# Moving the GLU, the gates and the SSM branch of a hybrid decoder layer, and the first expert's VectorE work

## The chip, the cores and the metric

One NeuronCore of a Trainium2 chip runs the whole layer in one launch. The metric is the device time in microseconds; the median of three runs is given, with the lowest and the highest. A profiled execution has its own time and a span, from its first instruction to its last.

## The reference, cut to what matters

The input is 1024 tokens of width 1024, with 16 meta tokens in front (L = 1040); all data are float32.

```
xn = RMSNorm(h)
[q | k | v | u | gate_a | gate_b] = xn @ W_in        # 512, 512, 512, 512, 1024, 1024 columns
a  = stick-breaking attention(q, k, v)               # 8 heads of 64, strictly causal
y  = gelu(S5 state-space model(u))                   # 32 groups of 16 channels, state 64
s  = y * sigmoid(y @ W_glu + b_glu)                  # the GLU, 512 columns
h += (sigmoid(gate_a) * (a @ W_pa) + sigmoid(gate_b) * (s @ W_pb)) @ W_o
h += mixture of 32 experts(RMSNorm(h))               # top 1 of 4 groups, then top 2 of 8 experts
out = RMSNorm(h), meta tokens dropped
```

## The kernel before, in words

Almost every product is made in three passes: each operand is split into a rounded high part and a low part (`split`, L99 to L102: a ScalarE copy, then a VectorE subtraction), and `mm3` (L132) adds high x high, high x low and low x high. Activations lie transposed, features on the 128 partitions, tokens along the columns. `load_w` (L144) loads a block of weights on SP's DMA queue into a page named `wr` and splits it into `wh` and `wl`; each name has two pages.

The stages, in order:

- `norms` (L192) takes the tokens in three groups of three tiles (tile 0 is the 16 meta tokens), normalizes each tile with `scale` (L124), either in one VectorE instruction or, where `NS` has a 1, by ScalarE and then GpSimd, and transposes it on TensorE into `xh` and `xl`. `ssm_in` projects u from them.
- `ssm_prep` and `ssm` (L370, L541) compute the state-space model, mostly on VectorE. Its result goes to memory (`y_d`). The generator `gates` (L176) is woven between its steps: 16 blocks of 128 gate columns, each two chunks of 512 tokens, 24 matmuls a chunk; a chunk's sigmoid is written to memory (`gate_d`). Its 32 chunks are dealt out: 21 to the state-space stage (`SF`), 3 with the first projections (`MF`), then 3, 3 and 2 to head pairs 0, 1 and 2 (`GP`).
- `att_proj` (L688) makes q, k, v of one pair of heads (eight chunks), `att_pair` (L752) the attention of a pair; `weave` (L57) runs the attention of one pair with the next pair's projections and the gate chunks. Pairs take turns on two sets of pages, `aq0` and `aq1`. Pairs 0 to 2 write their output to memory (`attn_d`), pair 3 straight into the pages `ah` and `al`.
- `glu` (L651) reads `y_d` back, splits it into `yh` and `yl`, and makes eight chunks of 12 matmuls, whose results it splits into `sh` and `sl`. Its pages lie where `xh` and `xl` lay, so that it starts when the last projection is done; it is woven with pair 3.
- The branch loop (L334 to L359) has eight blocks of 128 columns. For each it makes two chunks of `s @ W_pb` and two of `a @ W_pa`, 12 matmuls each; loads the gates `gb` and `ga` from `gate_d` (L347, L348, two pages each); VectorE multiplies each chunk by its gate (L349, L353), GpSimd adds the two (L354), and the sum is split into the pages `M` (L357). Between them the halves of W_o are loaded (`load_wo`).
- `out_proj` (L830) multiplies M by W_o tile by tile, normalizes, routes (`route`), and stores the rows for the experts (`hg_d`, L912).
- `moe` (L1017) runs the 32 experts. Their weights stream through a ring of twelve 1 MB pages on SP's queue; `unit` (L1083) splits one. The first expert's rows are gathered by an indirect DMA of GpSimd (`gather`, L1092) with the index `idx`, which the last routing step (`hold`, L1004) writes. The low parts of units (0, 1, 0) and (0, 0, 1) are put behind `hold` (L1106, L1219).

The order on each engine is laid down when the program is built: a planner takes the instructions by the order in which they are traced and by a model of their times, and each engine then runs its own list in order, waiting where data or a page is not there yet. From the first expert to the last (L1218) the order is written by hand for TensorE, ScalarE and VectorE. All ordinary DMAs stand in SP's list, and a wait there holds those behind it. TensorE's accumulators named `mm` are two.

Of the kernel before, what the change touches and what calls it, by code (L numbers as in the profile page):

```python
# [28 lines left out]
HD = 64  # L29
# [23 lines left out]
def _f(ap):  # L53
    return ap.bitcast(F32)
# [19 lines left out]
def tile_block(ctx, tc, i, out):  # L74
# [16 lines left out]
    attn_d = dr.tile([512, S], F32, name="attn_d")  # L91
    gate_d = dr.tile([2 * D, S], F32, name="gate_d")
# [46 lines left out]
    with ExitStack() as ca:  # L139
# [21 lines left out]
        with ExitStack() as cx:  # L161
# [14 lines left out]
            def gates(ms):  # L176
                for m in ms:
                    def ev_g(t, n0, n1):
# [3 lines left out]
                    yield from proj(2048 + m * 128, CH2, ev_g)  # L182


            gen = gates(range(16))
            with ExitStack() as c2:
                par = pool(c2, "par")
                with ExitStack() as c1:
# [3 lines left out]
                    def norms(lu, mark):  # L192
# [9 lines left out]
                        for g_, (t0, t1) in enumerate(NG):  # L202
# [11 lines left out]
                            for t in range(t0, t1):  # L214
# [35 lines left out]
                    drain(norms(lu, mark))  # L250
                    sp_ = ssm_prep(tc, par, i, bcast, prep)
# [18 lines left out]
            aq = [None, pool(c3, "aq1", bufs=2)]  # L270
            cq = ExitStack()
            aq[0] = pool(cq, "aq0", bufs=2)
            st = {}
            drain(islice(gen, MF), att_proj(tc, ap, aq[0], ps, proj, ident, 0, st))
            for hp in range(3):
# [3 lines left out]
                drain(fill, pair)  # L279
            dst = []  # L280
            pair = att_pair(tc, ap, ps, ident, 3, st, attn_d, dst)
            next(pair)
            drain(gen)
            cq.close()


        with ExitStack() as c4:
            c5 = ExitStack()
            p = pool(c5, "br", side="right")
            ah, al, sh, sl = (p.tile([128, 4, S], F32R, name=n) for n in ("ah", "al", "sh", "sl"))  # L290
            with ExitStack() as c6:
                nc.sync.dma_start(gb, i["glu_b"])
                at = pool(c6, "glu", bufs=2, side="right")
                gl = glu(tc, at, ps, i, load_w, mm3, split, gb, y_d, sh, sl)

                def loads():
                    for k in range(3):
                        a = wp.tile([128, 2, 512], F32, name="wr", bufs=2)
                        nc.sync.dma_start(a, attn_d[k * 128:k * 128 + 128])
                        split(ah[:, k], al[:, k], a.rearrange("p a b -> p (a b)"))  # L300
                        yield
                dst += ah, al
                weave(pair, chain(gl, loads()), 16, 18)
                drain(pair, gl)
# [29 lines left out]
            for m in range(KD):  # L334
                h, l = load_w([wb[:, :, m * 128:m * 128 + 128], wa[:, :, m * 128:m * 128 + 128]])
                T2 = []
                for q in range(2):
                    c = slice(q * 512, q * 512 + 512)
                    t = ps.tile([128, 512], F32, name="qk", bufs=2)
                    for k in range(4):  # L340
                        mm3(t, h[:, k, :], l[:, k, :], sh[:, k, c], sl[:, k, c], k == 0, k == 3)
# [1118 lines left out]
```

## Time and profile before

| | us |
|---|---|
| median of three runs | 1493.29 |
| lowest, highest | 1492.08, 1495.57 |
| profiled execution | 1491.31 |
| its span | 1489.6 |
| TensorE busy in the span | 1411.4 |
| VectorE, ScalarE, GpSimd busy | 1078.4, 798.7, 411.1 |

The span starts at 0. In the profile PE is TensorE's matmuls, PEld its weight loads, DVE VectorE, ACT ScalarE, POOL GpSimd, SPq the DMA queue of SyncE. A stretch is written as 525:575, in us from the span's start; PE's idle time in it is its length less PE's busy time. The granted clock of TensorE is given as a share of 2.4 GHz.

### The profile page before, as it was taken

The numbers are of one execution on the slowest core, as the hardware profiler recorded it, in microseconds if no ns is written. First come the engines' busy times: TensorE is split into PE (matmuls) and PEld (weight loads), VectorE is DVE, ScalarE is ACT, GpSimd is POOL, SyncE is SP. The second block draws the span as 40 slices with busy tenths as digits, with TensorE's granted clock in tenths as the row PEclk, the third lists the DMA queues.
The fourth block names the chain that finished last, engine by engine and source line by source line (L and its number), as shares of the span: only waits on it lengthen the run. The fifth ranks groups of instructions, "written<-read, shape, count | busy, mean of one in ns | idle before, by whom it ended". The sixth has DMA issues, their size and how long they took to land. (4 is left out here: it accounts for less than half of the span.)

```text
span 1489.6 us, 19758 instructions
## 1 busy us (share of the span) xinstructions
PE 1411.4 (95%) x7028; PEld 1145.9 (77%) x7028; DVE 1078.4 (72%) x1592; ACT 798.7 (54%) x1173; POOL 411.1 (28%) x367
## 2 busy tenths in 40 slices
PE   7989899999999978999999699999999999999994
PEld 5977788999999967778788577777777777777762
DVE  6799996475757677565577587777777777777747
ACT  6222222465656676432223277777777777777743
POOL 1161411135445564332254321111111111111033
PEclk8998999999999999999999899999999999999998
DMA  8232443211121014354863499999999999999753
GB/s 257 73 86 86 100 111 84 64 47 51 29 62 37 28 53 127 93 183 149 301 241 128 171 372 376 374 366 367 363 377 364 379 377 367 371 380 371 298 220 148
DMA packets 131749, 313.87 MB, mean 211 GB/s; under 512 B 27889, under 2 KB 81777, under 8 KB 107074
## 3 DMA queue, kind: packets, MB, share of 16 engines
q1 hardware_dynamic: 120450, 295.07, 55.3%
q0 software_dynamic: 9728, 16.83, 3.0%
q8 instruction: 56, 0.92, 0.3%
q10 hardware_dynamic: 1472, 0.69, 0.2%
q14 instruction: 43, 0.35, 0.1%
HBM read 284.03 MB, written 44.11 MB: 220 GB/s over the span
## 5 line engine op out<-in xcount | busy, mean ns | idle before, releaser
L136 PE MATMUL mm<-xh,wl 128*128 128x512 f32 (+4 forms) x608 | 220.7, 363 | 6.0 <-DVE wl L102 6.0
L134 PE MATMUL mm<-xh,wh 128*128 128x512 f32 (+4 forms) x608 | 221.5, 365 | 1.3 <-DVE kl L710 0.7
L135 PE MATMUL mm<-xl,wh 128*128 128x512 f32 (+4 forms) x608 | 220.7, 363 | 0.2 <-DVE xl L225 0.2
L136 PEld LDWEIGHTS mm<-xh,wl 128*128 128x128 f32 x608 | 115.0, 189 | 20.4 <-DVE wl L102 7.2
L134 PEld LDWEIGHTS mm<-xh,wh 128*128 128x128 f32 x608 | 114.8, 189 | 16.1 <-PE mm L136 1.6
L135 PEld LDWEIGHTS mm<-xl,wh 128*128 128x128 f32 x608 | 114.7, 189 | 13.1 <-DVE xl L225 0.7
L779 DVE TENSOR_TENSOR_SCAN pr<-pr 128x144 f32<-128x144 f32 (+3 forms) x64 | 91.2, 1426 | 41.8 <-POOL pr L776 40.6
L1173 POOL DMA_INDIRECT ye_d<-w,tab x32 | 33.4, 1042 | 270.4 <-ACT w L1166 269.8
L1089 DVE TENSOR_TENSOR w<-m,w 128x2048 fp32r<-128x2048 f32 x40 | 90.8, 2284 | 16.4 <-ACT w L1088 14.2
L1089 DVE TENSOR_TENSOR w<-r,w 128x2048 fp32r<-128x2048 f32 x40 | 91.3, 2284 | 15.4 <-ACT w L1088 15.4
L1095 POOL DMA_INDIRECT w<-hg_d,tab x31 | 41.2, 1331 | 211.5 <-PE tr L1116 203.1
L780 POOL TENSOR_TENSOR be<-be,pr 128x143 f32<-128x143 f32 (+3 forms) x64 | 86.7, 1358 | 41.2 <-DVE pr L779 39.1
L102 DVE TENSOR_TENSOR xl<-tr,xh 128x512 fp32r<-128x512 f32 x64 | 44.0, 687 | 65.2 <-ACT xh L101 57.9
L101 ACT CAST xh<-tr 128x512 fp32r<-128x512 f32 x64 | 37.6, 588 | 83.9 <-PE tr L1116 83.9
L102 DVE TENSOR_TENSOR wl<-wr,wh 128x1024 fp32r<-128x1024 f32 (+1 forms) x44 | 58.3, 1325 | 28.9 <-ACT wh L101 28.8
L101 ACT CAST wh<-wr 128x1024 fp32r<-128x1024 f32 (+1 forms) x44 | 44.5, 1011 | 63.7 <-PE mm L135 50.9
L1088 ACT CAST w<-r 128x2048 fp32r<-128x2048 f32 x40 | 76.3, 1907 | 3.0 <-PE mm L893 2.2
L1129 PE MATMUL a<-w,xh 128*128 128x512 f32 x196 | 77.8, 397 | 0.0
L1088 ACT CAST w<-m 128x2048 fp32r<-128x2048 f32 x40 | 76.5, 1912 | 0.7
L1131 PE MATMUL a<-w,xl 128*128 128x512 f32 x196 | 76.6, 391 | 0.0
L1130 PE MATMUL a<-w,xh 128*128 128x512 f32 x196 | 76.4, 390 | 0.0
L1166 ACT ACTIVATE w<-o,tab 128x512 f32<-128x512 f32 x64 | 44.2, 690 | 53.1 <-PE o L1159 53.1
(554 smaller groups left out, 3918.0 us busy)
## 6 DMA issues: line engine op xcount, KB each, us to landing
r<-in_w_dram SPq DMA_DIRECT2D x96, 1024.0 KB, 8.7
m<-in_w_dram SPq DMA_DIRECT2D x96, 1024.0 KB, 7.5
wr<-in_w_in_dram SPq DMA_DIRECT2D x32, 512.0 KB, 4.1
gate_d<-gt SPq DMA_DIRECT2D x32, 256.0 KB, 2.8
m<-ye_d SPq DMA_DIRECT2D x12, 512.0 KB, 8.6
x<-in_x_dram SPq DMA_DIRECT2D x8, 512.0 KB, 4.9
y<-y_d SPq DMA_DIRECT2D x16, 256.0 KB, 3.3
wr<-in_w_out_dram SPq DMA_DIRECT2D x8, 512.0 KB
```

What stands on the lines that cost most here:

```text
L101: a = (A if heng is None else heng).copy(h, src)
L102: return a.ins, (V if leng is None else leng).tensor_sub(l, src, _f(h)).ins
L134: nc.tensor.matmul(ps, lhsT=wh, rhs=xh, start=first, stop=False)
L135: nc.tensor.matmul(ps, lhsT=wh, rhs=xl, start=False, stop=False)
L136: nc.tensor.matmul(ps, lhsT=wl, rhs=xh, start=False, stop=last)
L779: V.tensor_tensor_scan(rv, rv, rv, 1.0, op0=OP.mult, op1=OP.bypass)
L780: P.tensor_mul(be[:, :W - 1], be[:, :W - 1], pr[:, 1:W])
L1088: A.copy(h, raws[n])
L1089: low = lambda: V.tensor_sub(l, raws[n], _f(h))
L1129: nc.tensor.matmul(acc[e][w], lhsT=xh[:, kk], rhs=h[:, k], start=(kk == 0), stop=False)
L1130: nc.tensor.matmul(acc[e][w], lhsT=xh[:, kk], rhs=l[:, k], start=False, stop=False)
L1131: nc.tensor.matmul(acc[e][w], lhsT=xl[:, kk], rhs=h[:, k], start=False, stop=(kk == KD - 1))
```

## The change

- `NS`: tile 1 is normalized by VectorE instead of ScalarE and GpSimd, and tile 0 comes last in the first group.
- `gates` has its weights loaded and split two blocks ahead (`weights(m + 2)`) for blocks 0 to 11 (`GA = 12`); the first two are asked for before `ssm_prep`. Blocks 12 to 15 are loaded in place. The chunks are dealt out as 21, 3, then 2, 2 and 2 to pairs 0 to 2, and the last 2 (`GL`) to pair 3.
- `glu` runs behind the first projections, in pages of its own; the set `aq1` is opened after it. Its results are stored to memory (`s_d`) with one page name (`gt`) shared with the gates.
- At pair 3 the rows of `s_d` are loaded and split (`load_s`) into pair 2's q, k and V pages, two gate chunks follow, woven over the first 4 of the pair's 16 steps. Over the other 12 run the 16 chunks of the SSM branch (`early`): each is multiplied by its gate and the product is written over the gate in `gate_d`. The rows of `attn_d` are loaded there too. Of pair 3, the first head's output now goes through `attn_d`.
- The branch loop makes the attention chunks alone; it loads both `gate_d` tiles for each chunk, and its weights come for two blocks at a time, two blocks ahead.
- The low parts of the units (0, 1, 0) and (0, 0, 1) of the first expert come later: the first behind a flag, which GpSimd writes after the first gather and VectorE copies, the second behind the first expert's own split.

The diff, without the renamings and the new page's declaration:

```diff
-NS = 0, 1, 0, 0, 1, 0, 0, 1, 0
+NS = 0, 0, 0, 0, 1, 0, 0, 1, 0
+GA = 12
-SF, MF, GP = 21, 3, (3, 3, 2)
+SF, MF, GP, GL = 21, 3, (2, 2, 2), 2
...
+            def gates():
+                def weights(m):
+                    return load_w([win[:, :, 2048 + m * 128:2176 + m * 128]])
+
+                ws = [weights(m) for m in range(2)]
+                yield
+                for m in range(16):
+                    if m >= GA:
+                        ws.append(weights(m))
+                    h, l = ws.pop(0)
+                    for n0, n1 in CH2:
+                        t = ps.tile([128, 512], F32, name="mm", bufs=2)
+                        for k in range(KD):
+                            mm3(t, h[:, k, :], l[:, k, :], xh[:, k, n0:n1], xl[:, k, n0:n1], k == 0, k == KD - 1)
                         gt = gp.tile([128, 512], F32, name="gt")
                         A.activation(gt, t, AF.Sigmoid)
                         nc.sync.dma_start(gate_d[m * 128:m * 128 + 128, n0 - NM:n1 - NM], gt)
+                        if n1 == L and m + 2 < GA:
+                            ws.append(weights(m + 2))
+                        yield
...
-                            for t in range(t0, t1):
+                            for t in chain(range(max(t0, 1), t1), range(t0, 1)):
...
                     drain(norms(lu, mark))
+                    next(gen)
                     sp_ = ssm_prep(tc, par, i, bcast, prep)
...
+            aq = [pool(c3, "aq0", bufs=2), None]
+            with ExitStack() as c6:
+                nc.sync.dma_start(gb, i["glu_b"])
+                gl = glu(tc, pool(c6, "glu", bufs=2, side="right"), gp, ps, i, load_w, mm3, split, gb, y_d, s_d)
+                next(gl)
+                drain(islice(gen, MF), att_proj(tc, ap, aq[0], ps, proj, ident, 0, st), gl)
+            aq[1] = pool(c3, "aq1", bufs=2)
...
             pair = att_pair(tc, ap, ps, ident, 3, st, attn_d, dst)
-            next(pair)
-            drain(gen)
-            cq.close()
+            pg = [aq[0].tile([128, n], F32R, name=nm, bufs=2)[:, :S] for n, nm in ((S, "qs"), (L, "kh"), (L, "kl")) for _ in range(2)]
+            vp = aq[0].tile([128, 9, 2, 2, HD], F32R, name="V", bufs=1).rearrange("p a b c d -> p (a b c d)")
+            pg += [vp[:, n * S:n * S + S] for n in range(2)]
+            sh, sl = pg[:4], pg[4:]
+
+            def load_s(src, h, l, k, n=128):
+                a = wp.tile([128, 2, 512], F32, name="wr", bufs=2)[:n]
+                nc.sync.dma_start(a, src[k * 128:k * 128 + n])
+                split(h[k][:n], l[k][:n], a.rearrange("p a b -> p (a b)"))
...
+            fill = chain(rows(), islice(gen, GL))
+            weave(pair, fill, 4, GL + 4)
+            drain(fill)
...
+            p = pool(c5, "gat", side="right", bufs=2)
...
+            def gate(row, m, q):
+                g = p.tile([128, 512], F32, name="ga" if row else "gb")
+                d = gate_d[row * D + m * 128:row * D + m * 128 + 128, q * 512:q * 512 + 512]
+                nc.sync.dma_start(g, d)
+                return g, d
+
+            def early():
+                for m in range(KD):
+                    if m % 2 == 0:
+                        w = load_w([wb[:, :, (m + n) * 128:(m + n) * 128 + 128] for n in range(2)])
+                    for q in range(2):
+                        g, d = gate(1, m, q)
+                        V.tensor_mul(g, g, branch(m, q, *(x[:, m % 2 * 4:m % 2 * 4 + 4] for x in w), sh, sl, "mm"))
+                        nc.sync.dma_start(d, g)
                         yield
+                    if m < 4:
+                        load_s(attn_d, ah, al, m, 128 if m < 3 else 64)
+
+            fill = early()
+            weave(pair, fill, 12, 2 * KD)
+            drain(pair, fill)
...
+            nxt = weights(0)
             for m in range(KD):
-                h, l = load_w([wb[:, :, m * 128:m * 128 + 128], wa[:, :, m * 128:m * 128 + 128]])
+                at = m % 2 * 4
+                if not at:
+                    w, nxt = nxt, weights(m + 2) if m + 2 < KD else None
                 for q in range(2):
...
+                    (g_, _), (ga, _) = gate(1, m, q), gate(0, m, q)
+                    V.tensor_mul(ga, ga, branch(m, q, *(x[:, at:at + 4] for x in w), ah, al, "mm"))
+                    P.tensor_add(ga, ga, g_)
                     for r in range(2):
                         mh, ml = M[2 * q + r]
                         split(mh[:, m], ml[:, m], ga[:, r * 256:r * 256 + 256])
...
-            split(sh[:, m, c], sl[:, m, c], sg.rearrange("p c t -> p (c t)"))
+            nc.sync.dma_start(s_d[m * 128:m * 128 + 128, q * 512:q * 512 + 512], sg.rearrange("p c t -> p (c t)"))
...
         with tc.issue_after(rt["hold"]):
-            unit(0, 1, 0)
+            lows = [unit(0, 1, 0, later=True), unit(0, 0, 1, later=True)]
...
         gather(0)
+
+        flag = p.tile([128, 2], F32, name="flag", bufs=1)
+        with tc.issue_after(first[0]):
+            P.memset(flag[:, 0:1], 0.0)
+        with tc.issue_after(rt["hold"]):
+            go = V.tensor_copy(flag[:, 1:2], flag[:, 0:1]).ins
+        with tc.issue_after(go):
+            lows[0]()
         x = [xparts(xt(0, 0), 0), None]
         tp = xt(0, 1)
         x[1] = xparts(tp, 1)
         A.copy(xf, tp)
+        with tc.issue_after(x[1][1]):
+            lows[1]()
...
-            with tc.issue_after(rt["hold"]):
-                unit(0, 0, 1)
```

## Rows read from the trace of the kernel before

**Rows 1.** The page: engines' busy time, and one row of its DMA issues.

```profile
PE 1411.4 (95%) x7028; PEld 1145.9 (77%) x7028; DVE 1078.4 (72%) x1592; ACT 798.7 (54%) x1173; POOL 411.1 (28%) x367
...
r<-in_w_dram SPq DMA_DIRECT2D x96, 1024.0 KB, 8.7
```

**Rows 2.** By windows: length, busy us of each engine, granted clock, DMA share, GB/s.

```profile
300.00:525.00 225.00, 223.40 (x1402) 207.04 (x1402) 146.20 (x203) 138.38 (x327) 105.11 (x124) 1.00 0.14 42
525.00:575.00 50.00, 37.97 (x224) 31.27 (x223) 38.26 (x42) 34.99 (x87) 34.61 (x42) 0.97 0.20 64
575.00:635.00 60.00, 58.48 (x289) 48.13 (x287) 37.13 (x37) 32.48 (x67) 17.81 (x18) 1.00 0.40 115
635.00:707.00 72.00, 70.08 (x303) 56.50 (x304) 44.69 (x66) 19.93 (x40) 21.54 (x14) 1.00 0.53 172
...
825.00:845.00 20.00, 8.05 (x49) 6.01 (x49) 11.75 (x54) 3.47 (x6) 6.17 (x5) 0.73 0.70 250
845.00:1432.00 587.00, 585.26 (x2524) 442.74 (x2522) 454.44 (x318) 421.43 (x376) 78.51 (x67) 1.00 0.92 351
```

**Rows 3.** Timeline, 10 to 23 us: start, duration, engine, line, operation, shapes.

```profile
10.30 1.27 DVE L130 SCALAR_TENSOR_TENSOR xn<-x,rr,g 16x1024 f32<-16x1024 f32 x1
...
12.42 2.50 POOL L128 TENSOR_TENSOR xn<-xn,g 128x1024 f32<-128x1024 f32 x1 [10.93 <-ACT xn L127]
12.75 3.24 DVE L130 SCALAR_TENSOR_TENSOR xn<-x,rr,g 128x1024 f32<-128x1024 f32 x1
...
22.72 1.29 DVE L130 SCALAR_TENSOR_TENSOR xn<-x,rr,g 128x1024 f32<-128x1024 f32 x1
```

**Rows 4.** Timeline, 107 to 117 us: TensorE, and VectorE's weight split.

```profile
107.24 0.40 PE L134 MATMUL mm<-xh,wh 128*128 128x512 f32 x1
107.47 0.39 PE L135 MATMUL mm<-xl,wh 128*128 128x512 f32 x1
...
109.11 3.19 DVE L102 TENSOR_TENSOR wl<-wr,wh 128x1024 fp32r<-128x1024 f32 x1
...
112.35 0.80 PE L136 MATMUL mm<-xh,wl 128*128 128x512 f32 x1 [4.48 <-DVE wl L102]
116.14 1.97 PE L590 MATMUL tr<-ident,ET 128*128 128x128 f32 x8 [2.99 <-DVE ET L584]
```

**Rows 5.** Waits of TensorE, 525:575: total, times, longest.

```profile
PE mm L135 <- DVE yl L102: 4.6, 3, 2.1
```

**Rows 6.** DMA issues, 600:707: count, size, median us from issue to landing.

```profile
gb<-gate_d SPq DMA_DIRECT2D x16, 256.0 KB, 3.7
ga<-gate_d SPq DMA_DIRECT2D x16, 256.0 KB, 5.4
```

**Rows 7.** Timeline of the branch loop: gate pages on VectorE and SP's queue.

```profile
639.67 0.32 SPq L348 DMA_DIRECT2D ga<-gate_d  x1
...
642.72 0.69 DVE L353 TENSOR_TENSOR ga<-ga,mm 128x512 f32<-128x512 f32 x1 [1.27 <-DMA ga<-gate_d]
...
684.69 0.68 DVE L353 TENSOR_TENSOR ga<-ga,mm 128x512 f32<-128x512 f32 x1
...
688.37 0.42 DVE L102 TENSOR_TENSOR m<-ga,m 128x256 fp32r<-128x256 f32 x1
...
688.82 0.32 SPq L348 DMA_DIRECT2D ga<-gate_d  x1
```

**Rows 8.** Timeline, 831 to 847 us: the first gather and what runs beside it.

```profile
831.21 4.50 DVE L1089 TENSOR_TENSOR w<-r,w 128x2048 fp32r<-128x2048 f32 x2
833.56 2.52 SPq L1079 DMA_DIRECT2D r<-in_w_dram  x2
834.02 2.61 POOL L1095 DMA_INDIRECT w<-hg_d,idx  x1 [7.15 <-DVE eps L1303]
...
842.41 1.94 PE L1116 MATMUL tr<-ident,w 128*128 128x128 f32 x8 [6.60 <-DMA w<-hg_d,idx]
...
846.43 1.05 POOL L1095 DMA_INDIRECT w<-hg_d,tab  x1 [7.19 <-ACT xf L1209]
```

More of the change, by code (lines that the diff above doesn't have):

```diff
@@ L91, in tile_block @@
     attn_d = dr.tile([512, S], F32, name="attn_d")
+    s_d = dr.tile([512, S], F32, name="s_d")
     gate_d = dr.tile([2 * D, S], F32, name="gate_d")
@@ L181, in ev_g @@
                         nc.sync.dma_start(gate_d[m * 128:m * 128 + 128, n0 - NM:n1 - NM], gt)
-                    yield from proj(2048 + m * 128, CH2, ev_g)
-            gen = gates(range(16))
+                        if n1 == L and m + 2 < GA:
+                            ws.append(weights(m + 2))
+                        yield
+            gen = gates()
             with ExitStack() as c2:
@@ L281, in tile_block, with rows @@
             pair = att_pair(tc, ap, ps, ident, 3, st, attn_d, dst)
-            next(pair)
-            drain(gen)
-            cq.close()
+            pg = [aq[0].tile([128, n], F32R, name=nm, bufs=2)[:, :S] for n, nm in ((S, "qs"), (L, "kh"), (L, "kl")) for _ in range(2)]
[6 more added lines that the diff above has]
+                split(h[k][:n], l[k][:n], a.rearrange("p a b -> p (a b)"))
+            def rows():
+                for k in range(4):
+                    load_s(s_d, sh, sl, k)
+                    yield
+            fill = chain(rows(), islice(gen, GL))
+            weave(pair, fill, 4, GL + 4)
+            drain(fill)
         with ExitStack() as c4:
@@ L289, in tile_block @@
             p = pool(c5, "br", side="right")
[L290 to L300, printed above, removed]
-                        yield
-                dst += ah, al
-                weave(pair, chain(gl, loads()), 16, 18)
-                drain(pair, gl)
+            ah, al = ([x[:, k] for k in range(4)] for x in (p.tile([128, 4, S], F32R, name=n) for n in ("ah", "al")))
@@ new lines, in tile_block, with branch @@
+            p = pool(c5, "gat", side="right", bufs=2)
+            wa, wb = (i[n].rearrange("(k p) c -> p k c", p=128) for n in ("w_branch_attn", "w_branch_ssm"))
+            def branch(m, q, h, l, h_, l_, name):
+                c = slice(q * 512, q * 512 + 512)
+                t = ps.tile([128, 512], F32, name=name, bufs=2)
+                for k in range(4):
+                    mm3(t, h[:, k], l[:, k], h_[k][:, c], l_[k][:, c], k == 0, k == 3)
+                return t
+            def gate(row, m, q):
[3 more added lines that the diff above has]
+                return g, d
@@ L648, in ssm, with glu @@
                                         ap=[[S, CH], [CH * S, 8], [1, 128]]), Y[ti * CH:ti * CH + CH])
-def glu(tc, p, ps, i, load_w, mm3, split, gb, y_d, sh, sl):
+def glu(tc, p, gp, ps, i, load_w, mm3, split, gb, y_d, s_d):
     nc = tc.nc
@@ L824, in att_pair @@
                     r = slice(64 * e, 64 * e + 64)
[L825 to L826 removed]
+                    A.copy(ah[hp][r, c], po[r])
+                    V.tensor_sub(al[hp][r, c], po[r], _f(ah[hp][r, c]))
                 yield
```

45 lines of the change are left out of this document (10 added, 35 removed).

## The prediction

> **What bounds the kernel now.** I read the profile's head first: TensorE is busy for 95% of the span [rows 1]. The view by windows then shows where the rest lies, as the length of a stretch less PE's busy time [rows 2]. The expert stage has 1.7 us idle in 587 and the pairs 1.6 in 225: both are bound by TensorE, nothing in the diff reduces its work, and a start or seam that gets shorter is therefore kept to the end. The idle time is in islands: 12.0 us at 525:575, 12.0 at 825:845 [rows 2], and two waits of together 7.5 in the SSM stage [rows 4]. The branch products at 635:707 have 1.9. A chunk of gate projection is 24 matmuls of 512 columns, which start 0.23 us apart [rows 4], so 5.5 us; a GLU or branch chunk is 12 of them, 2.75 us. The change moves such chunks into the islands. What I looked for is whether each place that gives up chunks can spare them.
>
> **The change part by part**, minus meaning faster.
>
> *Start, -1.5.* Tile 1 is normalized on ScalarE and GpSimd until 12.42 + 2.50 = 14.92; in the same time VectorE's own tile takes 3.24 us where it takes 1.29 with GpSimd quiet [rows 3]. After the change VectorE does tile 1 in about 1.29, then tile 2 without the slow-down, and the 16-row tile 0 last. Both ends: 3.3 us (14.92 less 10.3 + 1.29, if VectorE starts tile 1 at 10.3 as it now starts tile 0 [rows 3]) and 0, if weights and later tiles arrive no sooner. I take less than half, since all u chunks still need four weight splits in the same queue.
>
> *SSM stage, -4.* PE waits 4.48 us for the low part of a gate weight, whose subtraction is queued on VectorE among the SSM's products until 109.11 + 3.19, then 2.99 us for ET [rows 4]. With weights loaded two blocks ahead (SP and ScalarE work moves with them, 512 KB and one cast each) the first wait goes. What is late next is ET: VectorE is in order and has the same work ahead of it, so PE may reach the ET transposes 4.5 us sooner and wait there longer. Ends: -7.5 and 0; I take the middle.
>
> *GLU behind the first projections, +1.5.* Its y splits held PE for 4.6 us in the last pair [rows 5]. In the new place three gate chunks and eight projection chunks run ahead of it, which hide y loads and splits; if that cover fails, 4.6 comes back. The eight results go to memory (eight stores of 256 KB) and return as four loads of 512 KB; eight splits of 512 columns become four of 1024. Pairs 0 and 1 each lose one gate chunk of fill: +1, between 0 and 5.5 (one chunk's cover gone), near the 1.6 that pairs show now [rows 2].
>
> *Last pair's seam, -11.* At 525:575 PE has 12.0 us without work [rows 2], and its longest wait is for the GLU's y [rows 5], because the projections are used up and the GLU's pages come free late. Two gate chunks (11.0 us) now stand there. The SSM rows cannot do it: their splits go into pair 2's q, k and V pages, the last free only after pair 2's last product. Ends: -12.0, and 0 if the planner spends these chunks earlier. I take what the two chunks hold.
>
> *SSM branch beside the last heads, +1.* Sixteen chunks with VectorE's product (0.68 [rows 7]) and a store of each gated tile; a gate page is loaded (3.7 [rows 6]), multiplied and stored, and its next load waits on SP for that store, with weights and attention stores queued behind. Two pages give two chunks per turn; PE has attention between the chunks, so I see cover; without it up to 6. The head that now goes through memory adds four 64 KB stores and one load with its split.
>
> *Attention branch alone, +16.* This is the term that decides. The gate tiles still have two pages each. Follow one page: product at 684.69, then GpSimd's sum and two splits, the last low part from 688.37 to 688.79, next load on SP at 688.82 [rows 7]: 4.1 us. The load takes 3.7 us (one gate) or 5.4 (the other) in the median [rows 6], 3.05 at the least, from 639.67 to the product that waited for it at 642.72 [rows 7]. So a page turns in 4.1 + 3.7 = 7.8 us and serves one chunk in two. Today two chunks of attention and two of SSM branch run in that time, 11.0 us, and the turn hides. With the SSM half gone PE needs 5.5, and no other PE work is left to cover it: the output projection needs all eight blocks. Two pages are full at the start, so seven turns cost 7 x 2.3 = 16. Ends: 3.05 gives 7.15 and +12; 5.4 gives 9.5 and +28. I take 3.7, since per 7.8 us the DMA moves no more than now. The SSM rows (2 MB) and the gated tiles (4 MB) are each written and read once more than now, some 12 MB of extra traffic, in stages whose DMA share is 0.40 and 0.53 [rows 2]: room enough.
>
> *Start of the experts, -6.* The first gather is issued at 834.02 and takes 2.61 us, while two low-part subtractions run from 831.21 to 835.71; a later gather takes 1.05 [rows 8]. Each subtraction also frees a page, and SP at once sends two loads of 1 MB [rows 1], from 833.56 on, ahead of the gather's rows; these reach PE at 842.41, 5.8 us after the instruction's end [rows 8]. With the subtractions put behind a flag that GpSimd writes after the gather, I count 1.55 for the instruction, 2.7 for the landing (5.8 less the 3.05 of a load with little ahead), and some 1.7 for a shorter pause, since the granted clock in 825:845 is 0.73, part of it at the 1.2 GHz level [rows 2]. Ends: -1.5 and -8. The deferred low parts are 2.3 each and lie beside PE's first 24 matmuls. The issue time itself stays: the gather waits for the last stored rows.
> By the Trainium skill, "SBUF — State Buffer", section "Who interferes with whom", a tensor_tensor with two SBUF inputs holds up only GpSimd's reads, and descriptor generation, which writes, would not be held (marked there as inferred). The gather at 834.02, 2.61 against 1.05, speaks against it [rows 8]; by the page 1.55 of the 6 would not come and the sum would be -1.5.
>
> **Sum:** -1.5 - 4 + 1.5 + 1 - 11 + 1 + 16 - 6 = -3. The profiled execution took 1491.3 us, 2.0 below the median of the runs; 1488.3 for such an execution is 1490.3 for the median. A change within 0.2% (3.0 us) can't be told from none here.
>
> **Rivals.** *The pages turn fast enough (24%).* If the attention branch costs its lower end, 12, and the islands go nearly whole (SSM -7.5, start -3.3, experts -8, with seam -11 and 3.5 for the rest), the sum is -14, 1479. For it: the 3.05 row, and fewer products per time on VectorE. Against: that row has PE waiting for the page in a stage with twice the cover.
> *The gate pages bind harder, and the kernel is slower (24%).* One mechanism: the load of a gate at 5.4 as its median is now, a turn of 9.5, +28 instead of +16, sum +9, 1502. It decides from a turn of 8.2 us on, where 7 x 2.7 eats the 19 that the rest brings. For it: both gates of a chunk are loaded now one behind the other, each SP wait holds the queue. Against: fewer weights per time.
> *The seam stays (10%).* The planner lets pairs 0 and 1 use the spare gate chunks, and the rows wait for pair 2's pages, so the change does not put gates beside the last heads: 0 instead of -11, sum +8, 1501.
>
> **Numbers.** The forecast, the sum as worked, has 42%, own range -9 to +4, 1484 to 1497: 19 of it faster by over 0.2%, 17 within, 6 slower. The fast rival is faster throughout. Of the slower one 22 is slower and 2 within, of the seam's 8 and 2. Faster 0.43, same 0.21, slower 0.36. For 8 in 10 the range reaches towards both rivals, 1476 to 1506.
>
> **What would show it.** At 525:575 PE idle should drop from 12 to a few us; the gap before ET may stay. In the attention branch stage, about 60 us instead of 44, PE should wait for VectorE's gate product once per chunk or two, and SP's gate loads should start right behind the last low part. The first gather should take about 1.05 and PE resume 3 to 6 us after it. If the branch stage runs dense the forecast is too slow by 16; if the seam's idle time stays, too fast by 11.

## The result, and the profile after the change

The changed kernel takes 1534.45 us in the median of four runs (1530.74 to 1535.69); the kernel before took 1492.78 beside it (1492.08 to 1495.57). The ratio is 1.0269, 95% interval 1.0251 to 1.0286: slower by 42 us, where 3 us faster was forecast and the range ended at 1506. The profiled execution took 1534.28 us, its span is 1532.6.

The page's row of busy times, kernel after:

```profile
PE 1434.4 (94%) x7028; PEld 1161.0 (76%) x7028; DVE 1080.7 (71%) x1587; ACT 798.9 (52%) x1169; POOL 406.0 (26%) x367
```

Against [rows 1] the span is 43.0 us longer. TensorE's idle time (span less busy) went from 78.2 to 98.2, and the same 7028 matmuls are busy for 23.0 us more. So about half of the loss is not idle time but matmuls at the lower granted clock (mean 0.982 before, 0.967 after), which the windows show in the stretches that hold long waits. Kernel after, by windows (columns as in [rows 2]):

```profile
258.00:300.00 42.00, 37.52 (x197) 34.06 (x195) 24.11 (x36) 20.96 (x43) 6.54 (x13) 0.92 0.35 101
...
300.00:550.00 250.00, 245.66 (x1510) 225.42 (x1510) 166.59 (x221) 150.21 (x348) 108.65 (x126) 1.00 0.21 60
550.00:600.00 50.00, 40.39 (x192) 33.88 (x191) 26.93 (x28) 26.60 (x60) 25.73 (x27) 0.83 0.24 76
600.00:670.00 70.00, 68.33 (x346) 56.73 (x344) 36.00 (x35) 30.95 (x69) 25.00 (x30) 1.00 0.55 172
670.00:738.00 68.00, 54.71 (x213) 42.21 (x214) 41.60 (x56) 22.07 (x42) 20.27 (x14) 0.92 0.57 187
738.00:785.00 47.00, 36.48 (x176) 30.09 (x176) 21.29 (x75) 7.64 (x20) 14.20 (x14) 0.93 0.71 270
863.00:885.00 22.00, 14.16 (x72) 10.51 (x73) 13.64 (x68) 2.17 (x6) 7.45 (x8) 0.69 0.62 207
885.00:1477.00 592.00, 585.98 (x2509) 440.80 (x2508) 453.82 (x318) 421.66 (x376) 75.83 (x67) 0.99 0.92 351
```

Read beside [rows 2]. The pairs (300:550) have 4.3 us idle where they had 1.6. The seam (550:600) still has 9.6 where it had 12.0, at a lower clock. The last pair with the SSM branch (600:670) is dense. The attention branch (670:738) has 13.3 idle and takes 68 us. The output projection's first 47 us have 10.5 idle, and the expert stage after its first transposes 6.0 where it had 1.7. The first projections (258:300) have 4.5; the same stretch of the kernel before has 1.0 (40.96 busy of 42, clock 1.00).

TensorE's waits, kernel after, in 100:130, 258:300, 670:740 and 740:785 (total us, times, longest):

```profile
PE tr L632 <- DVE ET L626: 7.9, 1, 7.9
...
PE qk L811 <- ACT kh L749: 3.1, 1, 3.1
...
PE mm L136 <- DVE gb L395: 12.7, 7, 3.3
...
PE tr L946 <- DVE h L939: 8.8, 1, 8.8
PE mm L936 <- DVE gb L395: 1.7, 1, 1.7
```

One wait of 7.9 us for ET stands where two of together 7.5 stood [rows 4]. The waits for the gate product and the 8.8 us at the first sum of the output projection are new. (In the changed code the page named gb holds the attention gate, ga the gated SSM tile.)

In what follows a difference between two kernels is the difference of their ratios to the kernel before, times 1493 us. Each ratio's interval is about 0.002 to either side, less where five rounds were run, so such a difference is good to about 4 us.

### The profile page after: what moved, and what is told of

Its sections match the earlier page's. It is cut to its first block, busy times and chain, and to the rows that moved or that the text cites. A ratio compares the mean times of both kernels' runs of the same rounds, so it can differ in the third digit from the quotient of the medians.

```text
span 1532.6 us, 19841 instructions
## 1 busy us (share of the span) xinstructions
PE 1434.4 (94%) x7028; PEld 1161.0 (76%) x7028; DVE 1080.7 (71%) x1587; ACT 798.9 (52%) x1169; POOL 406.0 (26%) x367
## 5 line engine op out<-in xcount | busy, mean ns | idle before, releaser
L821 POOL TENSOR_TENSOR be<-be,pr 128x143 f32<-128x143 f32 (+3 forms) x64 | 91.7, 1437 | 38.4 <-DVE pr L820 36.1
```

The costliest lines, as they stand in the source:

```text
L821: P.tensor_mul(be[:, :W - 1], be[:, :W - 1], pr[:, 1:W])
```

## Experiments: gate pages, and the queue ahead of x

**e1_pages.**

```diff
-            p = pool(c5, "gat", side="right", bufs=2)
+            p = pool(c5, "gat", side="right", bufs=4)
```

> The changed kernel with four pages for each of the two gate tiles of the branch stage instead of two, nothing else. Theory (page turn): in the changed kernel PE waits 12.7 us in seven waits for VectorE's gate product in the stage 670:738, because a page turns in about 8 us and two pages serve two chunks of 2.75 us. Four pages serve four chunks, 11 us, so the seven waits go: 10 to 18 us less than 1534.5, that is 1517 to 1525, and the longest wait for the gate product in that stage is below 1 us. Rival (the transfers are what is short, not the pages): the loads arrive no sooner, the waits stay, and the time stays within 1530 to 1537.

Measured: 1520.19 us, ratio 1.0173 (1.0155 to 1.0191), 14 us less than the change. The turn of a page in the changed kernel, by the timeline (gate product, next load, next product):

```profile
697.20 0.69 DVE L395 TENSOR_TENSOR gb<-gb,mm 128x512 f32<-128x512 f32 x1 [2.59 <-DMA gb<-gate_d]
...
702.04 0.32 SPq L339 DMA_DIRECT2D gb<-gate_d  x1
...
705.14 0.69 DVE L395 TENSOR_TENSOR gb<-gb,mm 128x512 f32<-128x512 f32 x1
...
710.86 0.34 SPq L339 DMA_DIRECT2D gb<-gate_d  x1
...
714.69 0.68 DVE L395 TENSOR_TENSOR gb<-gb,mm 128x512 f32<-128x512 f32 x1
```

7.94 and 9.55 us for a turn that serves two chunks of together 5.5. The part from a product to the page's next load took 4.84 and 5.72 us, the load 3.10 and 3.83. With four pages TensorE's waits in 670:738 are:

```profile
PE mm L136 <- DVE gb L395: 4.2, 7, 0.9
```

and the clock in that stretch is 1.00. The pages were what was short, and not the loads. What is left is seven waits of at most 0.9 us for the same product.

**e3_x_first.**

```diff
         for n in range(6):
-            load(n)
+            with tc.issue_after(rt["xl"][1]):
+                load(n)
```

> The changed kernel with the first six raw loads of expert weights (1 MB each) made to wait for the second load of x of the output projection. Theory (queue order): at 738.69 six loads of 1 MB are issued ahead of the x loads, x lands at about 760 and PE waits 8.78 us for the sum that needs it. With x ahead the wait goes: 6 to 9 us less, 1525 to 1529, and the first experts start no later because their weights have 100 us to arrive. Rival (the wait is elsewhere: x waits for a page, or the delayed expert loads are then missing at the experts' start): 1531 to 1540.

Measured: 1528.67 us, ratio 1.0238 (1.0215 to 1.0261), some 5 us less than the change. SyncE's queue in the changed kernel, by the timeline:

```profile
738.69 3.76 SPq L1123 DMA_DIRECT2D r<-in_w_dram  x6
742.50 3.02 SPq L922 DMA_DIRECT2D h<-in_x_dram  x2
```

and in this run:

```profile
735.84 4.18 SPq L922 DMA_DIRECT2D h<-in_x_dram  x2
```

The wait for the sum drops from 8.8 to 2.0 us. In the changed kernel six raw pages come free together as the branch stage ends (SyncE's last wait ahead of the six loads is for a branch product), and six loads of 1 MB then stood ahead of x. In the kernel before, x was asked for first:

```profile
707.17 0.81 SPq L878 DMA_DIRECT2D h<-in_x_dram  x2
...
716.83 9.93 SPq L1079 DMA_DIRECT2D r<-in_w_dram  x6
```

## Experiments: the last pair's seam

**e2_gates_first** turns the order of the fill round; **e10_gates_in_hole** does that and holds the first product of each of the two chunks behind an output of pair 2; **e14_chunks_given_back** has no chunk there at all.

```diff
-            fill = chain(rows(), islice(gen, GL))
+            fill = chain(islice(gen, GL), rows())
...
+                            with (tc.issue_after(st["pv"][-2 if n1 < L else -1]) if m == 15 and k == 0 else ExitStack()):
```

```diff
-SF, MF, GP, GL = 21, 3, (2, 2, 2), 2
+SF, MF, GP, GL = 21, 3, (3, 3, 2), 0
```

> The changed kernel with the order of the last pair's fill turned round: the two gate chunks first, then the four loads of SSM rows. Theory (the rows hold the weight pages): the row loads take the two raw weight pages and cannot be split before pair 2's pages come free at 573, so the gate block's weights are loaded only at 575 and its chunks run after 581, when the idle time is over. With the gates first their weights come during pair 2, the two chunks stand in the idle time at 550:580, and 6 to 11 us go: 1523 to 1528. Rival (the order only moves the wait): the rows then come after the gates and the SSM branch waits for them at 597, or the chunks are taken by pair 2, and the time stays within 1531 to 1537.

Measured: 1541.6 us, ratio 1.0327 (1.0305 to 1.0349): 9 us slower than the change, outside both expectations. The rows did hold the weight pages; kernel after, by the timeline:

```profile
573.68 2.45 DVE L104 TENSOR_TENSOR V<-wr,kh 128x1024 fp32r<-128x1024 f32 x2 [1.92 <-PE pv L853]
575.02 0.39 SPq L152 DMA_DIRECT2D wr<-in_w_in_dram  x1
```

The low parts of two SSM rows go into pair 2's V page, wait for its last product (pv), and until then hold both raw weight pages (wr); the gate block's weights are issued 1.3 us after the first of these splits begins. The chunks ran from 581.5 to 597.1, behind the idle time. But with the gates first, their weights came early and the chunks ran at 546 to 564, inside pair 2. The idle time moved behind them, with one wait of 4.1 us that ends at 572.65. Either order misses the hole. The 9 us are not lost at the seam: in its trace the attention branch begins at 669.66, in the changed kernel's at 670.51. What costs them behind it is not shown.

> The changed kernel with the gates first in the last pair's fill, and the first product of each of the two last chunks held behind the end of pair 2's last but one and last output. With the gates first and not held they ran at 545 to 563, inside pair 2, and the idle time moved to 564:588. Theory (the hole needs the chunks between pair 2's last products and the SSM rows): held, they fill it, idle time at 550:600 drops from about 9 to 2 us and the SSM branch starts at about 588: 5 to 8 us less than the changed kernel, 1526 to 1530. Rival (what ends this stage is the chain of pair 3's heads through VectorE, ScalarE and GpSimd, so the idle time only moves on): 1532 to 1540, as with the gates first.

Measured: 1529.17 us, ratio 1.0234 (1.0214 to 1.0255), 5 us less than the change and 14 less than the same order unheld. The chunks ran at 564 to 571 and 575 to 581. By windows:

```profile
550.00:575.00 25.00, 20.75 (x125) 17.64 (x124) 16.43 (x22) 17.17 (x41) 16.67 (x19) 0.93 0.13 42
575.00:600.00 25.00, 24.59 (x126) 20.68 (x125) 17.19 (x15) 14.58 (x30) 7.85 (x11) 1.00 0.63 197
```

4.7 us idle in 550:600, half of the 9.6, where 2 was expected, and the attention branch begins at 665.53, 5.0 us sooner than in the changed kernel. The two chunks fill about half of the seam if they stand in it. (Against e2 the branch begins 4.1 us sooner, so the seam explains no more than that of the 14.)

> The changed kernel with the two last gate chunks back in pairs 0 and 1 (three, three and two chunks of fill as before the change) and none beside the last heads. Theory (in the changed kernel the two chunks at 581:597 cover the SSM rows' loads and splits, and the two pairs lose 3 us without them): pairs 3 us faster, the stretch up to the SSM branch 4 to 11 us longer in idle time, in sum 1 to 8 us slower than the changed kernel, 1535 to 1542. Rival (the chunks cover nothing where they stand, after the idle time): 2 to 4 us faster, 1530 to 1533.

Measured: 1541.57 us, ratio 1.0322 (1.0303 to 1.0341), 8 us slower than the change. So even late the chunks are worth something. The pairs (300:550) are 1.2 us less idle (246.87 busy), where 3 was expected. The attention branch begins at 673.66, 3.2 us later than in the changed kernel, and the span is 6.2 us longer; the other half of that is spread over the stages behind and not explained.

## Experiments: the GLU behind the first projections

**e9_glu_rows_later** puts the y splits behind five projection chunks in the order of the code; **e13_glu_rows_held** holds them behind the first V eviction.

```diff
-                next(gl)
-                drain(islice(gen, MF), att_proj(tc, ap, aq[0], ps, proj, ident, 0, st), gl)
+                pj = att_proj(tc, ap, aq[0], ps, proj, ident, 0, st)
+                drain(islice(gen, MF), islice(pj, 6))
+                with tc.issue_after(st["vf"]):
+                    next(gl)
+                drain(pj, gl)
```

(e9 has 5 for 6, and next(gl) without the order.)

> The changed kernel with the GLU's y loads and splits issued behind the first five projection chunks of pair 0 instead of ahead of all eight. Theory (ScalarE in order): at 276 ScalarE stands 1.4 us on a y tile that has not landed, with the eviction of Q and K behind it, PE waits 3.1 us and then runs at the lower clock; with the y splits later the stretch 258:300 loses 2 us as before the change and not 8: 3 to 6 us less, 1528 to 1532. Rival (the y splits are in the way wherever they stand: the GLU's own chunks then wait for them): the wait moves to 300:335 and the time stays within 1532 to 1537.

Measured: 1536.65 us, ratio 1.0291 (1.027 to 1.0312), no gain. The trace shows why this told nothing: the y loads were still issued right behind the y stores, at 268.29, and the splits still stood at 271 to 281. Moving the lines in the code did not move the work: the planner still put it where its inputs were ready.

> The changed kernel with the GLU's y loads and splits held behind the eviction of pair 0's first V chunk. (The run with the y splits behind five chunks left them at 271:281, so it did not test this.) Theory: the y splits at 271:278 stand in ScalarE's order ahead of the evictions of Q and K, PE waits 3.1 us and then runs at the lower clock; held, the stretch 258:300 loses 2 to 3 us instead of 8, and the GLU, which starts at 305 in the changed kernel, has its splits by then: 4 to 6 us less, 1528.5 to 1530.5. Rival (the splits then stand in the way of the GLU's chunks or of pair 0's evictions, and the loss moves to 300:345): 1532 to 1537.

Measured: 1530.01 us, ratio 1.023 (1.0211 to 1.0248), 6 us less than the change. ScalarE in the changed kernel, by the timeline:

```profile
276.38 0.62 ACT L103 CAST yh<-y 128x512 fp32r<-128x512 f32 x1 [1.36 <-DMA y<-y_d]
...
277.79 0.58 ACT L741 CAST qs<-mm 64x512 fp32r<-64x512 f32 x1
...
278.86 0.44 ACT L749 CAST kh<-mm 64x352 fp32r<-64x352 f32 x1
```

It stands on a y tile that has not landed, with the eviction of Q and K behind it; TensorE had ended those chunks at 276.2 and waits until 279.35. Held, by windows:

```profile
258.00:300.00 42.00, 41.39 (x240) 38.14 (x239) 22.88 (x36) 21.18 (x45) 6.50 (x13) 1.00 0.25 76
```

0.6 us idle at the full clock, and in 300:345, where the GLU then stands, 1.0.

## Experiments: gate weights and the start, each alone

**e5_gates_alone** is the kernel before with the change's gate generator (weights two blocks ahead), **e6_start_alone** with its start:

```diff
-NS = 0, 1, 0, 0, 1, 0, 0, 1, 0
+NS = 0, 0, 0, 0, 1, 0, 0, 1, 0
...
-                            for t in range(t0, t1):
+                            for t in chain(range(max(t0, 1), t1), range(t0, 1)):
```

> The kernel before with one part of the change alone: the gate projections' weights loaded and split two blocks ahead; order and number of the chunks stay. The prediction's term: 4 us faster, ends 7.5 and 0. The reading of the two traces: the 4.5 us wait for the low part of a weight goes, the wait for ET grows from 3.0 to about 8, because VectorE's queue is what both wait for, and 0 to 2 us are left, ratio 0.999 to 1.000. Rival (the wait is worth what it lasts): ratio 0.996 to 0.998.

Measured: 1494.1 us against 1494.99, ratio 1.0000 (0.9991 to 1.0009): worth nothing. TensorE's waits in 100:130, of this run:

```profile
PE mm L137 <- DVE wl L103: 4.5, 1, 4.5
PE tr L605 <- DVE ET L599: 3.3, 1, 3.3
```

and of the run with the start alone:

```profile
PE tr L590 <- DVE ET L584: 7.9, 1, 7.9
```

So it is not the early weights that took the wait for the low part away in the changed kernel: with them alone it stays at 4.5. The start alone turns the two waits into one. In each case 7.5 to 7.9 us are spent waiting for VectorE's queue.

Asking for the weights two blocks ahead moved nothing here. The cast of the block in question, in the kernel before and in e5:

```profile
96.09 1.05 ACT L101 CAST wh<-wr 128x1024 fp32r<-128x1024 f32 x1 [4.68 <-PE mm L135]
```

```profile
96.36 1.05 ACT L102 CAST wh<-wr 128x1024 fp32r<-128x1024 f32 x1 [4.68 <-PE mm L136]
```

In both it waits until TensorE gives back one of the two pages of `wh`, and the low part's split stands behind the same SSM products, at 109.11 [rows 4] and at 109.38. Two pages are all the lead there can be, and the kernel before already had it.

> The kernel before with the change of the start alone: tile 1 scaled on VectorE, the 16-row tile 0 last of its group. The prediction's term: 1.5 us faster, ends 3.3 and 0. The reading of the two traces: the first 58 us lose 3.4 us more than before, so 2 to 4 us slower, ratio 1.0015 to 1.0025. Rival (the loss in the first 58 us comes from the gates' early weights, which the change issues there too): ratio 0.998 to 1.000.

Measured: 1493.13 us, ratio 0.9987 (0.9975 to 0.9999): no loss, and less than can be told from no change. The trace of this run is behind at 58 us (269 matmuls by then, 290 in the kernel before), and its span is 2.0 us longer than that of before, yet its times are not. **e18_mended_old_start**, below, put the two readings to the test.

## Experiments: the start of the experts

**e4_experts_back** is the changed kernel without this part.

> The changed kernel with the start of the experts as before the change (no flag, the two low parts of the first weights run ahead of the first gather again). Theory (the traces' idle time: the gather got 1.6 us shorter and came 4 us sooner to PE, but a new wait of 3.9 us for the second expert's rows took more than that): 1 to 4 us faster than the changed kernel, 1530 to 1533.5. Rival (the quiet VectorE does bring the 6 us of the prediction and the loss is elsewhere): 4 to 7 us slower, 1538 to 1542.

Measured: 1531.81 us, ratio 1.0252 (1.0235 to 1.0269). 2.5 us less than the change is within what the measurement leaves open; 4 us slower, as the rival had it, is not.

**e7_experts_alone** is the kernel before with this part; **e8_experts_after_put** moves the flag behind the last two scatters:

```diff
-        with tc.issue_after(first[0]):
-            P.memset(flag[:, 0:1], 0.0)
+        def flagged(q):
+            with tc.issue_after(q):
+                P.memset(flag[:, 0:1], 0.0)
...
         with tc.issue_after(q):
             put()
+        flag(puts[-1])
```

> The kernel before with the change of the experts' start alone: the two low parts of the first weights behind a flag that GpSimd writes after the first gather. The prediction's term: 6 us faster, ends 1.5 and 8. The reading of the two traces: the gather comes some 4 us sooner, the second expert's gather comes later by as much, and a wait of 3.9 us stands in its place: 0 to 3 us slower, ratio 1.000 to 1.002. Rival (the loss in the changed kernel is made by the earlier stages, and alone the part brings what was forecast): ratio 0.994 to 0.998.

> As the run with the experts' start alone, with the flag written after the last two scatters of the routing table instead of after the first gather, so that the deferred low parts do not run beside those scatters. Theory (the scatter of 3.1 us beside a subtraction, where one takes 1.0 alone, makes the second gather late): both scatters take about 1.0 us, the second expert's rows come some 2 us sooner than in the run beside it, and it is 1 to 3 us faster than that run, ratio 0.998 to 1.000. Rival (the second gather waits for the 1 MB weight loads ahead of it, not for the scatters): no difference between the two runs, or slower, since PE waits for the low part.

Measured: alone 1498.26 us, ratio 1.0028 (1.0018 to 1.0037), slower; with the flag behind the scatters 1490.97, ratio 0.9977 (0.9965 to 0.999), faster. Timeline of the first:

```profile
833.92 1.04 POOL L1095 DMA_INDIRECT w<-hg_d,idx  x1 [7.23 <-DMA hg_d<-hg]
...
835.17 2.28 DVE L1089 TENSOR_TENSOR w<-r,w 128x2048 fp32r<-128x2048 f32 x1
835.26 3.09 POOL L1009 DMA_INDIRECT tab_d<-pay,rows  x1 [0.19 <-issue]
837.52 0.33 SPq L1079 DMA_DIRECT2D r<-in_w_dram  x1
...
838.19 1.06 PE L1116 MATMUL tr<-ident,w 128*128 128x128 f32 x8 [3.03 <-DMA w<-hg_d,idx]
...
843.97 0.32 SPq L938 DMA_DIRECT2D tab<-tab_d  x1
...
851.94 1.08 PE L1116 MATMUL tr<-ident,w 128*128 128x128 f32 x4 [6.40 <-DMA w<-hg_d,tab]
```

and of the second:

```profile
837.67 0.96 POOL L1010 DMA_INDIRECT tab_d<-pay,rows  x1 [0.30 <-issue]
...
839.78 0.32 SPq L939 DMA_DIRECT2D tab<-tab_d  x1
...
841.29 0.79 PE L1117 MATMUL tr<-ident,w 128*128 128x128 f32 x4 [1.58 <-DVE ov L929]
...
842.26 1.04 POOL L1096 DMA_INDIRECT w<-hg_d,tab  x1 [3.52 <-DMA tab<-tab_d]
843.44 2.29 DVE L1090 TENSOR_TENSOR w<-r,w 128x2048 fp32r<-128x2048 f32 x1
```

The first gather did what was forecast: 1.04 us instead of 2.61, and its rows reach TensorE at 838.19 instead of 842.41 [rows 8]. But the deferred subtraction now ran beside the next instruction in GpSimd's queue, a scatter of the routing table, which took 3.09; the subtraction's end freed a page, and a load of 1 MB went out at 837.52 ahead of the read of the table. That read waits on SyncE for the scatters to land, 6.4 us after their issue in the median against 2.5 in the second run, and was issued 5.3 us after the last scatter began, against 2.1. (That the load in flight slows the landing is inferred.) TensorE waited 6.4 us for the second expert's rows, and the clock fell: 0.56 in 852:858, against 1.00 in the second run. In the changed kernel the same chain costs 3.9 us at 890.39.

**e16_put_and_count** also puts VectorE's count of rows ahead of the first deferred subtraction; **e17_both_held** in addition holds the second one behind the second gather with the same flag.

```diff
+            if n == 1:
+                with tc.issue_after(first[1]):
+                    P.memset(flag[:, 0:1], 0.0)
+                with tc.issue_after(x[1][1]):
+                    go = V.tensor_copy(flag[:, 1:2], flag[:, 0:1]).ins
+                with tc.issue_after(go):
+                    lows[1]()
```

> The kernel before with the experts' start, the flag behind the last scatters, and the flag's copy on VectorE also behind its count of rows per expert. Theory: with the flag behind the scatters PE's first expert transposes waited 1.6 us at 841 for that count, which stood on VectorE behind the deferred subtraction of 2.3 us. With the count ahead this wait goes, and the low part comes about 1 us later beside PE's first products: 1 to 2 us less than the ratio 0.9977 of that run, 0.996 to 0.997. Rival (the rows of the first gather land no sooner, the DMA wait takes its place): 0.997 to 0.999.

> The kernel before with the experts' start, both deferred subtractions held by flags: the first behind the last scatter and the count, the second behind the second expert's gather. Theory (a subtraction beside a gather's issue costs the gather 1.5 us and the rows behind it more): the second gather takes about 1.0 us, the wait for its rows at about 851 goes or is below 1 us, ratio 0.995 to 0.998. Rival (the second low part then comes too late and PE waits for it instead): a wait for the low part of 1 to 3 us at 846 to 850, ratio 0.999 to 1.004.

Measured: 1497.96 us, ratio 1.0028 (1.0016 to 1.004), and 1492.12, ratio 0.9982 (0.9971 to 0.9993). The first fell against its theory. The wait for the count is gone, as expected, but the second subtraction began 0.3 us sooner and the second gather 1.5 us later than in e8, and they met. The granted clock in 852:858 is 0.56 again, against 1.00 in e8. Timeline of e16:

```profile
843.12 2.29 DVE L1090 TENSOR_TENSOR w<-r,w 128x2048 fp32r<-128x2048 f32 x1
843.77 2.56 POOL L1096 DMA_INDIRECT w<-hg_d,tab  x1 [4.62 <-DMA tab<-tab_d]
...
851.79 1.09 PE L1117 MATMUL tr<-ident,w 128*128 128x128 f32 x4 [3.56 <-DMA w<-hg_d,tab]
```

and of e17:

```profile
844.03 1.04 POOL L1096 DMA_INDIRECT w<-hg_d,tab  x1 [4.35 <-DMA tab<-tab_d]
...
846.60 2.28 DVE L1090 TENSOR_TENSOR w<-r,w 128x2048 fp32r<-128x2048 f32 x1
846.69 3.06 POOL L1096 DMA_INDIRECT w<-hg_d,tab  x1 [0.19 <-issue]
848.58 0.63 PE L1117 MATMUL tr<-ident,w 128*128 128x128 f32 x4 [0.57 <-DMA w<-hg_d,tab]
```

With the order forced, the gather that TensorE waits for takes 1.04, the collision falls on a later one, and the gain is back (0.9982, at the slow end of what was expected). In e8 the gather had come 1.2 us ahead of the subtraction with nothing to hold it there: luck.

**e12_start_and_put** is e8 with the changed start.

> The kernel before with two parts: the start of the change, and the experts' start with the flag written behind the last scatters. The two alone gave ratios 0.9987 and 0.9977. If they add up: 0.996 to 0.997, faster than both kernels. Rival (the start alone brought nothing, as its trace says): 0.997 to 0.999.

Measured: 1492.27 us, ratio 0.9985 (0.9972 to 0.9998): the start adds nothing to e8.

## Experiments: the mends together

**e11_four_mended** has e1, e3, the flag of e8 and the edit of e9; **e15_all_mended** has e1, e3, e10, e13 and the edits of e16.

> The changed kernel with four of its waits mended together: four pages for each gate tile, x ahead of the expert weights, the flag behind the routing table's last scatters, and the y splits behind five projection chunks. If they add up: 14.3 and 5.8 us by their runs, 7.3 by the two runs on the experts' start, some 4 for the y splits, from 1534.5 to about 1503, ratio 1.006. Rival (they hide one another): 1510 to 1520. Either way the rest over the kernel before is what the change costs in the seam and in the branch stage without its cover.

> The changed kernel with six waits mended: four pages for each gate tile, x ahead of the expert weights, the flag behind the last scatters and VectorE's count of rows ahead of the deferred low part, the y splits held, and the two gate chunks first and held for the hole. If they add up: four gave 1506.0; 5 to 8 for the hole, 4 to 6 for the y splits and 1.5 for the count, in sum 1491 to 1495.5, ratio 0.998 to 1.001. Rival (the y splits or the hole do not add): 1497 to 1504.

Measured: 1506.0 us, ratio 1.0079 (1.0059 to 1.0099); and 1493.63, ratio 0.9995 (0.9982 to 1.0007). The edit of e9 moved nothing in e11 either (258:300 has 37.15 us busy, as in e9), so three mends count there: 27 us by their own runs (14, 5 and the 8 between e7 and e8), against 28 measured. They add up.

Six take the ratio from 1.0269 to 0.9995. Of these 41 us the single runs give 14, 5, 5 and 6 (e1, e3, e10, e13). The edits of e16 brought nothing by themselves, but in e15 the second gather just came ahead of the subtraction:

```profile
842.70 1.07 POOL L1146 DMA_INDIRECT w<-hg_d,tab  x1 [3.54 <-DMA tab<-tab_d]
842.76 2.29 DVE L1140 TENSOR_TENSOR w<-r,w 128x2048 fp32r<-128x2048 f32 x1
```

So the experts' part went there as in e8, by 0.06 us and unforced, and counts with the same 8. In sum 38, within what they can be told to: the loss is accounted for. TensorE's clock is back at 0.98. By windows, e15:

```profile
665.00:725.00 60.00, 54.63 (x235) 42.67 (x234) 43.26 (x64) 22.72 (x46) 24.10 (x21) 1.00 0.73 243
```

But it ends level with the kernel before. One price that remains is in the branch stage, 5.4 us idle in these 60, of which 5.2 are six waits for VectorE's gate product.

> The mended kernel (ratio 0.9995) with the start as before the change. If the trace of the start alone is right (3.8 us behind at 58 us, not made good): 3 to 4 us faster, ratio 0.9965 to 0.998. If its times are right (0.1% faster than before): 0 to 2 us slower, ratio 0.9995 to 1.001.

Measured: 1492.72 us, ratio 0.9999 (0.9985 to 1.0012). By its times the changed start is worth nothing either way, here as in e6 and e12. By the traces it costs something: the three pairs that differ in it alone (e6 and the kernel before, e12 and e8, e15 and e18) have spans longer by 2.0, 2.6 and 3.1 us with it. These are single executions, and the two readings are not reconciled.

Three versions are faster than both kernels by their intervals, each by about 0.2%: e8 (0.9977), e17 (0.9982) and e12 (0.9985), the kernel before with the experts' start mended.

## Why the prediction was wrong, point by point

- **Attention branch alone, +16:** right in mechanism and nearly in size. Turns of 7.94 and 9.55 us were measured where 7.8 was worked out, the excess mostly ahead of the load (4.84 and 5.72, where 4.1 was taken) and not in it (3.10 and 3.83, where 3.7 was taken); the seven waits came, 12.7 us and 1.7 at the end; taking them away is worth 14. The stage took 68 us and not about 60, since the waits also cost clock (0.92) and some matmuls of the last pair still stand in it.
- **Last pair's seam, -11:** this step failed: "Two gate chunks (11.0 us) now stand there." They stood behind it, at 581.5 to 597.1. The prediction saw that the rows' splits wait for pair 2's pages, but did not ask what the rows hold while they wait: both raw weight pages, and with them the chunks' weights. At the seam 2.4 us of idle time went, at a clock of 0.83 instead of 0.97; forced into the hole, the chunks brought 5 us (e10).
- **Start of the experts, -6:** failed at its end. The gather and its rows came as worked out (4.2 us sooner in e7), but the term stopped at the first expert. The deferred low parts were costed as lying "beside PE's first 24 matmuls"; the first lay beside a scatter of GpSimd's and freed a page ahead of the table's read. Alone the part costs 0.28%, 4 us (e7); in the changed kernel taking it back brought 2.5 us, too little to tell from none (e4).
- **SSM stage, -4:** measured 0.0, within 0.1% (e5). The step "the first wait goes" failed: early weights left it at 4.5 us. By the traces two pages of `wh` allow no earlier cast, and the split behind it keeps its place in VectorE's queue. The end at 0 was right, and VectorE's queue, named there, is what both waits are for; but the wait was to move to ET because of the weights, and it moved with the changed start.
- **GLU, +1.5:** mis-sized. The price if the cover fails was named as 4.6; the cover was counted in TensorE's chunks, and it failed on ScalarE, where the y splits stood ahead of these chunks' own evictions. Holding the splits is worth 6 (e13).
- **x behind the expert loads:** not in the sum at all, some 5 us (e3). SyncE's order at the end of the branch stage was not followed into the output projection.
- **Pairs +1** was low (2.7 us more idle); **early SSM branch +1** was about right (1.7 idle in 70, where 575:635 had 1.5 in 60 [rows 2]); **start -1.5** can't be told from 0.

Rival "The seam stays" had the outcome at the seam and half of the condition: the rows did wait for pair 2's pages, but the chunks were not spent in pairs 0 and 1; they came late. It was priced with all else at the forecast, as each rival was. "The gate pages bind harder" looked for the excess in the loads, which came out near the 3.7 taken. Three gains of together 21 us were forecast and none came: the chunks missed the hole, the early weights moved nothing, and the gather's gain was lost in the transfers behind it. Beside them the GLU and x cost some 10 us where 1.5 was counted. Only the experts' term had a price for the clock at which TensorE works after a wait, and about half of the longer span is busy time at the lower clock.

The Trainium skill's "SBUF — State Buffer", section "Who interferes with whom", infers that a tensor_tensor with two SBUF inputs doesn't hold up descriptor generation. For the indirect DMAs of this case the traces differ: the four that began within 0.7 us of the start of such a subtraction, in the fences of e7, e16 and e17 and at 843.61 in e8, took 2.56 to 3.09 us, and those without one beside them 0.96 to 1.04. The measurement decides. These instructions also read an index (idx, rows, tab), and no run separates what they read from what they write.

## What to carry to other kernels

VectorE work that is moved out of the way of one GpSimd instruction can land in the way of the next: follow the order up to the last transfer that TensorE needs, and force it, since a shift of under 2 us decided between 0.2% faster and 0.3% slower. Filler work fills a hole only if it stands in it: ask which pages its weights need and who holds them. When half of a loop is moved elsewhere, what is left must still cover the turn of its pages; count pages per chunk before and after.

## What the runs showed of the hardware

An indirect DMA's instruction that begins during VectorE's 2.28 us subtraction ended 0.9 us after that subtraction ended, in every place looked at: in e7 it ends at 838.35, the subtraction at 837.45; in e16 at 846.33 and 845.41; in e17 at 849.75 and 848.88. These began 0.1 to 0.7 us into it; in e8 one that began 2.0 us into a subtraction, at 884.64, took 1.21 and ended 0.9 us after it as well. That is about the time one takes alone, as if it began when the subtraction ended. One that began 0.06 us ahead of the subtraction was not held: 1.07 us (e15). And waits cost twice: 20 us more of idle time came with 23 us more of busy time for the same matmuls, at a mean granted clock of 0.967 instead of 0.982.
